# Router tiles on the place of the merged activations, router products with tokens on the partitions, late modulation products behind the first gather

## The chip, the cores and the metric

The kernel runs on one core of a Trainium2 chip. A core has TensorE (PE in the rows; PEld is its loading of weights), VectorE (DVE), ScalarE (ACT), GpSimd (POOL) and SyncE (SP), which here only issues transfers; 16 DMA engines carry them. The metric is the device time of one execution in microseconds. Everything is float32 (some products run on pairs of rounded values).

## The reference

One layer over 256 tokens of width 2048: a token mixer, then a mixture of 32 experts in four groups, each with a residual, and a last norm. The part that the change touches is the second half's beginning.

```python
mod = cond @ ada_w[l] + ada_b[l]
sh1, sc1, g1, sh2, sc2, g2 = jnp.split(mod, N_MOD, axis=-1)
...
x = x + g1[:, None, :] * mixer(h, ...)
h = modulate(rmsnorm(x, norm2_g[l]), sh2, sc2)
x = x + g2[:, None, :] * hier_moe(h, ...)
...
def hier_moe(h, wg_r, bg_r, we_r, be_r, w_gate, w_up, w_down):
    g_probs = jax.nn.softmax((hf @ wg_r + bg_r).astype(jnp.float32), axis=-1)
    g_top_p, g_top = lax.top_k(g_probs, 1)
    e_logits = (hf @ we_r + be_r).astype(jnp.float32).reshape(t, N_GROUPS, EXPERTS_PER_GROUP)
    sel = e_logits[jnp.arange(t), g_top[:, 0]]
    l_top, l_idx = lax.top_k(sel, TOP_K)
    weights = g_top_p * jax.nn.softmax(l_top, axis=-1)
    experts = (g_top * EXPERTS_PER_GROUP + l_idx).astype(jnp.int32)
    y = grouped_expert_ffn(hf, experts.reshape(-1), weights.reshape(-1), w_gate, w_up, w_down)
```

Each expert computes (silu(x w_gate) * (x w_up)) w_down with inner width 512; a token goes to two experts of one group.

## The kernel before

**Stages.** Until about 641 us the kernel computes the modulation vectors (`ada1`, `ada2`, on VectorE from 512 KB blocks) and the mixer. The mixer's last stage is the output product: for each of four blocks of 512 columns (`cb`) eight blocks `mow` of 512 KB are split into a rounded part and a rest (`hi` on ScalarE, `lo` on VectorE) and multiplied with the merged activations `mh`, `ml`. `residual(cb)` adds the result into `x1` and sums squares into `ss2`; `router_part(cb)` transposes the new columns of `x1` and multiplies them with the 36 router columns `wra` into `plg`, for the first three column blocks in the middle of the next block's products, for the last one behind all of them.

**Router.** From `plg` come the logits `lg`, from them the choice of group and experts (`onehot`, two one-hot matrices whose sum is `ma`), a rank of each token within its expert (`rk`, from three small products of `ma` with a triangular table) and a weight (`ge`, `gp`, `w1`, `w2`, `wt`).

**Experts.** The 32 experts run as eight quads of four. `gather(q)` builds a 0/1 matrix `gt` from the ranks, multiplies it with `x1` (`ph`) and evicts the 16 pieces of `hq` in turn on ScalarE and VectorE, with the second norm and the modulation applied. `quad(q)` multiplies `hq` with 16 blocks of gate and up weights (`pg`, `pu`), then with 8 blocks of down weights (`pd`). Each block is one transfer `exw` of 2048 KB, 24 a quad, 192 in all, issued by SyncE.

**Where the blocks lie.** `ring` hands out slots: five in pool `wxa` (slots 0 to 4), two in `wxb` (5, 6), and slot 7 in `wx4`, used once; after the eighth block the order is 0 to 6 again. The blocks for slots 0 to 4 are loaded in quarters during the output product (`early_some`). `wxb` lies where `mh` and `ml` lay. `wx4` and the router's tiles (pool `rt2`) lie where the ring `wp` of eight 512 KB buffers lay. The last eight of these buffers hold modulation blocks (`late`), whose products on VectorE (line 223) give the second gate `ada_state[3]`, first read in `gate2()` at the end of the first quad's gate and up products.

**What sets the order.** Inside the output product the order of SyncE is written out (`manual_schedule`). Everywhere else a scheduler places instructions by its own simulated time; each engine then runs its list in that order, and waits at the head of the list on semaphores.

## Time and profile before

| what | us |
|---|---|
| median of three runs (lowest, highest) | 1601.78 (1601.13, 1602.49) |
| the profiled execution | 1598.41 |
| its span | 1596.6 |
| TensorE busy in the span | 1233.2 (77%) |
| VectorE busy | 679.3 (43%) |
| ScalarE busy | 349.7 (22%) |
| moved by DMA | 616.27 MB, 386 GB/s in the mean |

The table gives the busy time of the whole span. The two halves have different limits, so a stage is read from its own stretch. The profile also follows the chain that ended last: 47% of the span are waits for transfers, 38% TensorE.

### The profile page before, as it was taken

The page shows a single profiled execution, that of the slowest core. Times are in us where ns is not written, and L with a number is a line of the kernel's source. Part 1 is how long each engine was busy: PE and PEld are TensorE (multiplying, and loading weights), DVE is VectorE, ACT ScalarE, POOL GpSimd, SP SyncE. Part 2 cuts the span into 40 slices and gives each one's busy share as a digit, 9 for nine tenths or more (in the row PEclk, how much of TensorE's full clock was granted, in tenths as well). Part 3 has the DMA queues.
Part 4 walks back from the last instruction along what each step waited for, and adds up shares of the span by engine and source line. Part 5 has one row for each costly group of instructions (what it writes and reads, how often), then busy time and mean ns, then how long its engine had stood idle before and what let it go on. Part 6 is the DMA issues. An engine that isn't in the chain of part 4 may idle for free.

```text
span 1596.6 us, 20401 instructions
## 1 busy us (share of the span) xinstructions
PE 1233.2 (77%) x8430; PEld 745.9 (47%) x8430; DVE 679.3 (43%) x946; ACT 349.7 (22%) x535; POOL 43.6 (3%) x40
## 2 busy tenths in 40 slices
PE   4999999999999899679657567667567566556755
PEld 3989999999899777325112112112112112111111
DVE  6989999798887966603003002002002002002002
ACT  3543355444555343112000000000000000000002
POOL 0000000300002100000000000000000000000001
PEclk9999999999999999799889779789779889777878
DMA  9999999899997899699999999999999999999996
GB/s 360 389 337 339 352 359 365 273 328 369 329 346 267 318 409 380 261 427 426 427 426 427 428 427 426 427 426 427 426 427 428 427 427 426 417 427 426 425 428 280
DMA packets 89229, 616.27 MB, mean 386 GB/s; under 512 B 10037, under 2 KB 10341, under 8 KB 64937
## 3 DMA queue, kind: packets, MB, share of 16 engines
q1 hardware_dynamic: 87700, 611.10, 95.2%
q10 hardware_dynamic: 1252, 3.48, 0.6%
q8 instruction: 68, 1.11, 0.3%
q0 software_dynamic: 176, 0.31, 0.1%
q14 instruction: 33, 0.26, 0.0%
HBM read 611.71 MB, written 2.10 MB: 384 GB/s over the span
## 4 chain that ended last, share of the span: by engine, by line
DMA 47%; PE 38%; DVE 5%; issue 1%; ACT 1%; POOL 0%; DVEq 0%; POOLq 0%; ACTq 0%
DMA w<-exw 45%; PE acc L116 23%; PE pd L116 3%; PE m L116 2%; PE ph L116 2%; PE pg L116 2%; PE pu L116 2%; DMA w<-ada 2%; DVE lo L108 1%; DVE ada L223 1%; PE po L116 1%; PE at_u L116 1%; PE pr L116 0%; DVE t L600 0%; PE sp L116 0%
## 5 line engine op out<-in xcount | busy, mean ns | idle before, releaser
L116 PE MATMUL pg<-w,hq 128*32 128x512 f32 x1024 | 185.0, 777 | 217.0 <-DMA w<-exw 217.0
L108 DVE TENSOR_TENSOR lo<-w,hi 128x1024 fp32r<-128x1024 f32 x192 | 239.5, 1253 | 42.6 <-ACT hi L107 37.8
L107 ACT CAST hi<-w 128x1024 fp32r<-128x1024 f32 x192 | 200.8, 1051 | 229.2 <-PE acc L116 179.5
L790 DVE TENSOR_TENSOR act<-act,pu 128x512 f32<-128x512 f32 x8 | 5.5, 688 | 526.2 <-PE pu L116 526.2
L116 PE MATMUL acc<-hh,hi 128*128 128x256 f32 x768 | 212.1, 280 | 0.6 <-ACT hi L107 0.6
L116 PE MATMUL acc<-hl,hi 128*128 128x256 f32 x768 | 211.3, 278 | 0.0
L116 PE MATMUL acc<-hh,lo 128*128 128x256 f32 x768 | 205.7, 279 | 2.2 <-DVE lo L108 2.1
L116 PEld LDWEIGHTS pg<-w,hq 128*32 128x32 f32 x1024 | 25.0, 118 | 363.1 <-DMA w<-exw 345.3
L116 PE MATMUL pu<-w,hq 128*32 128x512 f32 x1024 | 190.0, 793 | 0.0
L223 DVE SCALAR_TENSOR_TENSOR ada<-w,condT,ada 128x1024 f32<-128x1024 f32 x124 | 162.1, 1314 | 13.1 <-DMA w<-ada 12.2
L116 PE MATMUL pd<-w,aT 128*32 128x512 f32 x1024 | 132.2, 630 | 37.0 <-DMA w<-exw 35.5
L116 PEld LDWEIGHTS acc<-hh,hi 128*128 128x128 f32 x768 | 145.3, 189 | 2.1 <-ACT hi L107 1.4
L116 PEld LDWEIGHTS acc<-hl,hi 128*128 128x128 f32 x768 | 145.1, 189 | 0.3 <-issue 0.2
L786 ACT ACTIVATE act<-pg 128x512 f32<-128x512 f32 x8 | 4.8, 597 | 637.3 <-PE pg L116 637.3
L116 PEld LDWEIGHTS acc<-hh,lo 128*128 128x128 f32 x768 | 141.2, 189 | 3.0 <-DVE lo L108 2.6
L116 PE MATMUL po<-yb,gwt 128*128 128x512 f32 (+1 forms) x132 | 75.0, 659 | 30.4 <-DVE yb L808 19.4
L116 PEld LDWEIGHTS pu<-w,hq 128*32 128x32 f32 x1024 | 43.0, 138 | 109.9 <-issue 108.2
L116 PEld LDWEIGHTS ph<-gt,x 128*128 128x128 f32 x512 | 65.2, 195 | 43.8 <-issue 25.6
L116 PEld LDWEIGHTS pd<-w,aT 128*32 128x32 f32 x1024 | 28.7, 112 | 114.7 <-issue 60.4
L215 DVE SCALAR_TENSOR_TENSOR w<-w,condR 128x1024 f32<-128x1024 f32 x64 | 77.7, 1219 | 9.1 <-ACT condR L197 7.4
L116 PE MATMUL ph<-gt,x 128*128 128x128 f32 x512 | 74.8, 288 | 7.1 <-ACT hq L756 3.5
L815 DVE TENSOR_TENSOR x<-x,po 128x512 f32<-128x512 f32 (+1 forms) x66 | 44.3, 671 | 79.8 <-PE po L116 79.8
(246 smaller groups left out, 1481.4 us busy)
## 6 DMA issues: line engine op xcount, KB each, us to landing
w<-exw SPq DMA_DIRECT2D x186, 2048.0 KB, 30.7
w<-ada SPq DMA_DIRECT2D x192, 512.0 KB, 5.8
w<-mixw SPq DMA_DIRECT2D x64, 512.0 KB, 5.6
w<-gatew SPq DMA_DIRECT2D x64, 512.0 KB, 5.4
w<-mow SPq DMA_DIRECT2D x32, 512.0 KB, 10.2
w<-exw SPq DMA_DIRECT2D x24, 512.0 KB, 10.2
w<-fow SPq DMA_DIRECT2D x16, 512.0 KB, 5.3
w<-now SPq DMA_DIRECT2D x16, 512.0 KB, 5.1
```

What stands on the lines that cost most here:

```text
L107: nc.scalar.copy(hi, src)
L108: nc.vector.tensor_tensor(lo, src, hi.bitcast(F32), op=OP.subtract)
L116: return nc.tensor.matmul(ps, lhsT, rhs, start=start, stop=stop, skip_group_check=True)
L215: nc.vector.scalar_tensor_tensor(w, w, 1.0, condR[:, 1024 * kh:1024 * kh + 1024], op0=OP.mult, op1=OP.mult, accum_out=dst)
L223: nc.vector.scalar_tensor_tensor(a, w, condT[:, kc:kc + 1], a, op0=OP.mult, op1=OP.add)
L786: nc.scalar.activation(at_[:, 0], pg, AF.Silu)
L790: nc.vector.tensor_tensor(at_[:, 1], at_[:, 0], pu, op=OP.mult)
L815: nc.vector.tensor_tensor(x2[:, tb, c], base[:, tb, c], po[:, 0:n], op=OP.add)
```

## The change

Six things are edited.

1. The pool `rt2` of the router's tiles moves from the right side of the memory to the left, ahead of `wxb`. It now lies where `mh` and `ml` lay, slot 5 behind it on the rest of that place, and slots 6 and 7 on the buffers of `wp`.
2. In `router_part` the operands of the router product change places: the transposed tokens are the stationary operand, the 36 columns go through, one product for each half of the tokens. `plg` then holds tokens on its partitions. The copy to `lgs`, its clearing on GpSimd and the two products with the selecting table `C_SELR` go; the table goes from the constants.
3. The transposes of one column block are all issued for the first 128 tokens, then for the second, into two banks.
4. The last square sum (`cb == 3`, second half of the tokens) is taken on VectorE.
5. The late modulation products, and with them the weight steps and counts of the router, are put behind the first gather's last eviction on VectorE (`issue_after`); the subtraction for `ge` goes there too.
6. The second gather's instructions are put behind the same eviction.

```diff
     def router_part(cb):
+
+        px = [mps() for _ in range(2)]
+        for tb in range(2):
+            for pr in range(2):
+                for i in range(2):
+                    kc = 4 * cb + 2 * pr + i
+                    nc.tensor.transpose(px[pr][:, T * i + P * tb:T * i + P * tb + P],
+                                        x1[:, tb, kc * P:kc * P + P], ident)
         for pr in range(2):
-            px = mps()
+            xt2 = s4([P, 2, T], "x1t")
+            nc.scalar.copy(xt2, px[pr].rearrange("p (a b) -> p a b", a=2))
             for i in range(2):
                 kc = 4 * cb + 2 * pr + i
                 for tb in range(2):
-                    nc.tensor.transpose(px[:, T * i + P * tb:T * i + P * tb + P],
-                                        x1[:, tb, kc * P:kc * P + P], ident)
-            xt2 = s4([P, 2, T], "x1t")
-            nc.scalar.copy(xt2, px.rearrange("p (a b) -> p a b", a=2))
-            for i in range(2):
-                kc = 4 * cb + 2 * pr + i
-                mm(plg[64 * i:64 * i + 36, 0:T], wra[:, kc, :], xt2[:, i, :], kc < 2, kc >= KC - 2)
+
+                    mm(plg[:, 36 * tb:36 * tb + 36], xt2[:, i, tb * P:tb * P + P], wra[:, kc, :],
+                       kc == 0 and tb == 0, kc == KC - 1)
...
+    rt, _rt2 = pool("rt2", reuse_waits="tile")
     wxb, _wxb = pool("wxb", reuse_waits="tile")
-    rt, _rt2 = pool("rt2", "right")
     wx4, _wx4 = pool("wx4", "right", reuse_waits="tile")
 
 
-    lgs = rt.tile([P, T], F32, name="lgs")
-    nc.gpsimd.memset(lgs, 0.0)
-    for i in range(2):
-        nc.vector.tensor_copy(lgs[64 * i:64 * i + 36, :], plg[64 * i:64 * i + 36, 0:T])
...
-    pl = mps()
-    for tb in range(2):
-        mm(pl[:, 36 * tb:36 * tb + 36], lgs[:, tb * P:tb * P + P], cst[:, C_SELR:C_SELR + 36], True, True)
...
     hg = gather(0, rk, 1)
+
+    behind, first_evict = ExitStack(), last_evict[0]
+    behind.enter_context(tc.issue_after(last_evict[0].ins))
     for go in late:
         go()
...
+    behind.close()
...
-        hg = gather(q + 1, rk, q % 2)
+        with tc.issue_after(first_evict.ins) if q == 0 else ExitStack():
+            hg = gather(q + 1, rk, q % 2)
```

The scheduler orders the rest anew. On SyncE, behind the output product, the blocks `exw` of the first quad stood like this before; `w_1052` is the last modulation block, `w_1102`, `w_1103`, `w_1104` go into slots 5, 6 and 7, `w_1105` to `w_1109` into slots 0 to 4 again, and the names in brackets are the semaphores that an instruction waits for:

```order
L103 DMA w_1052_7066<-ada2 128x1024 [waits DMAHW5_49,DVE_49]
L727 DMA w_1102_7327<-exw 128x4096 [waits DMAHW6_49,PE_49]
L727 DMA w_1103_7337<-exw 128x4096 [waits DMAHW7_49,PE_49]
L727 DMA w_1104_7347<-exw 128x4096 [waits DMAHW1_49,DMAHW2_49,DMAHW0_49,DVE_49]
L869 TENSOR_LOAD nri_7273 [waits DMAHW3_49,DMAHW4_49,DMAHW2_49,DMAHW5_49,DMAHW1_49,DMAHW6_49,DMAHW0_49,DMAHW7_49,DVE_49,Activation_49]
L869 ISA x2
L727 DMA w_1105_7357<-exw 128x4096 [waits PE_49]
```

Behind these, `w_1106` to `w_1109` followed. The same place of SyncE now, where `w_1101`, `w_1102`, `w_1103` go into slots 5, 6 and 7 and `w_1104` to `w_1108` into slots 0 to 4 again:

```order
L101 DMA w_1052_7078<-ada2 128x1024 [waits DMAHW5_49,DVE_49]
L726 DMA w_1104_7366<-exw 128x4096 [waits DMAHW6_49,PE_49]
L726 DMA w_1105_7376<-exw 128x4096 [waits DMAHW7_49,PE_49]
L726 DMA w_1106_7386<-exw 128x4096 [waits DMAHW0_49,PE_49]
L726 DMA w_1107_7396<-exw 128x4096 [waits DMAHW1_49,PE_49]
L726 DMA w_1108_7406<-exw 128x4096 [waits DMAHW2_49,PE_49]
L726 DMA w_1101_7336<-exw 128x4096 [waits DMAHW3_49]
L726 DMA w_1102_7346<-exw 128x4096 [waits DMAHW4_49,DVE_49]
L726 DMA w_1103_7356<-exw 128x4096 [waits DMAHW5_49,DVE_49]
L874 TENSOR_LOAD nri_7282 [waits DVE_49]
```

The five blocks that reuse slots 0 to 4, each of which waits for the last `pu` product on the block before it in its slot, moved ahead of the three for slots 5, 6 and 7; the two of slots 6 and 7 wait for the seventh and the eighth late modulation product.

On VectorE, from the last column block's residual (`t`, `x1`) to the router's first step (`sst`), before (`ada_854` is the second gate, its `w` the late blocks):

```order
L600 TENSOR_TENSOR t_1053_7068<-acc_1011_6869,g1r_846_5907 128x512
L223 SCALAR_TENSOR_TENSOR ada_854_5950<-w_1045_7052,condT_77,ada_854_5950 128x1024
L600 TENSOR_TENSOR t_1054_7072<-acc_1012_6870,g1r_846_5907 128x512
L601 TENSOR_TENSOR x1_6285<-x1_6285,t_1053_7068 128x512
L223 SCALAR_TENSOR_TENSOR ada_854_5950<-w_1046_7054,condT_77,ada_854_5950 128x1024
L601 TENSOR_TENSOR x1_6285<-x1_6285,t_1054_7072 128x512
L223 SCALAR_TENSOR_TENSOR ada_854_5950<-w_1047_7056,condT_77,ada_854_5950 128x1024
```

Five more late products (`w_1048` to `w_1052`) and then `sst` followed. The same place of VectorE now:

```order
L598 TENSOR_TENSOR t_1053_7080<-acc_1011_6877,g1r_846_5907 128x512
L598 TENSOR_TENSOR t_1054_7084<-acc_1012_6878,g1r_846_5907 128x512
L599 TENSOR_TENSOR x1_6285<-x1_6285,t_1053_7080 128x512
L599 TENSOR_TENSOR x1_6285<-x1_6285,t_1054_7084 128x512
L601 SCALAR_TENSOR_TENSOR t_1054_7084,ss2_6323<-x1_6285 128x512
L652 TENSOR_REDUCE sst_7122<-ss2_6323 128x2
L148 TENSOR_SCALAR rv_1059_7124<-sst_7122 128x2
```

The eight late products moved away from between the sums and the router.

They stand behind the first gather's last eviction on VectorE (the first row here), among the second gather's `gt` and the weight steps:

```order
L752 TENSOR_SCALAR hq_1089_7203<-ph_1093_7243,ab2_497_3444,ab2_672_4665 128x128
L221 SCALAR_TENSOR_TENSOR ada_854_5950<-w_1045_7064,condT_77,ada_854_5950 128x1024
L221 SCALAR_TENSOR_TENSOR ada_854_5950<-w_1046_7066,condT_77,ada_854_5950 128x1024
L827 TENSOR_TENSOR ge_1067_7147<-lg_7135,mx_1063_7138 128x8
L832 TENSOR_TENSOR ex_1096_7270<-mx_1077_7165,mx_1073_7155 128x2
L853 TENSOR_REDUCE cn_7190<-cn_7190 1x1
L741 TENSOR_TENSOR gt_1143_7589<-rk_1085_7182,cst_73 128x128 x2
```

Before, this eviction was followed by the third gather's `gt`; the weight steps, the counts and the second gather's `gt` moved from within the router's chain to this place.

## Rows read from the trace of the kernel before

**Rows 1.** Page, the span in 40 equal slices: GB/s moved by the DMA engines.

```profile
GB/s 360 389 337 339 352 359 365 273 328 369 329 346 267 318 409 380 261 427 426 427 426 427 428 427 426 427 426 427 426 427 428 427 427 426 417 427 426 425 428 280
```

**Rows 2.** Stretches: length, busy us of PE, PEld, DVE, ACT, POOL, clock, DMA share, GB/s.

```profile
800.00:1000.00 200.00, 132.43 (x820) 41.17 (x824) 27.34 (x56) 9.46 (x20) 0.00 (x0) 0.87 1.01 427
...
656.00:680.00 24.00, 17.65 (x126) 9.68 (x126) 10.15 (x54) 2.61 (x7) 0.74 (x2) 0.75 0.40 157
...
641.00:656.00 15.00, 5.64 (x24) 3.04 (x22) 14.34 (x24) 4.11 (x8) 0.31 (x1) 0.61 1.01 419
...
645.00:650.00 5.00, 3.48 (x14) 1.68 (x14) 5.00 (x6) 1.90 (x4) 0.00 (x0) 0.50 1.00 426
...
560.00:640.00 80.00, 77.05 (x355) 60.08 (x354) 49.06 (x47) 31.86 (x42) 0.00 (x0) 1.00 1.01 395
...
sum 520.00, PE 506.68 PEld 479.76 DVE 468.77 ACT 244.17 POOL 33.50; mean PE 84.45 PEld 79.96 DVE 78.13 ACT 40.69 POOL 5.58
```

**Rows 3.** SyncE: issues by start and duration; then one of its waits (us, times, longest).

```profile
637.31 12.34 SPq L727 DMA_DIRECT2D w<-exw  x3
...
669.82 28.61 SPq L727 DMA_DIRECT2D w<-exw  x11
...
SPq L727 <- DVE ada L223: 7.1, 1, 7.1
```

**Rows 4.** TensorE in order of time, 640 to 676: start, duration, what, [idle before].

```profile
641.31 0.39 PE L116 MATMUL acc<-lo,mh 128*128 128x512 f32 x1
...
645.77 1.54 PE L610 MATMUL m<-cst,x 128*128 128x128 f32 x6 [1.28 <-DVE x L601]
647.40 1.93 PE L116 MATMUL plg<-x1t,wr 128*36 128x256 f32 x8
...
660.59 1.76 PE L116 MATMUL m<-ma,cst 128*128 128x32 f32 x10 [5.15 <-DVE w L833]
...
668.71 1.03 PE L116 MATMUL pu<-w,hq 128*32 128x512 f32 x8
...
671.65 1.04 PE L116 MATMUL pu<-w,hq 128*32 128x512 f32 x8
```

**Rows 5.** The other engines in order of time; then four pieces of the chain.

```profile
640.83 0.69 DVE L600 TENSOR_TENSOR t<-acc,g1r 128x512 f32<-128x512 f32 x1 [3.97 <-PE acc L116]
...
642.63 0.68 DVE L600 TENSOR_TENSOR t<-acc,g1r 128x512 f32<-128x512 f32 x1
643.23 0.68 DVE L601 TENSOR_TENSOR x<-x,t 128x512 f32<-128x512 f32 x1
...
645.03 0.68 DVE L601 TENSOR_TENSOR x<-x,t 128x512 f32<-128x512 f32 x1
...
645.63 7.26 DVE L223 SCALAR_TENSOR_TENSOR ada<-w,condT,ada 128x1024 f32<-128x1024 f32 x6
...
646.76 1.17 ACT L613 COPY x1t<-m 128x512 f32<-128x512 f32 x2 [0.23 <-PE m L610]
...
653.00 0.31 POOL L645 MEMSET lgs<- 128x256 f32 x1 [102.79 <-DVE ada L223]
...
655.48 0.42 DVE L656 SCALAR_TENSOR_TENSOR lg<-m,rr,cbr 128x36 f32<-128x36 f32 x2 [0.30 <-PE m L116]
...
656.29 0.07 DVE ge L678
...
660.45 0.08 DVE w L833
...
662.78 0.66 DVE gt L742 x3
...
666.15 0.43 PE pt L767 x2
```

**Rows 6.** TensorE at full clock: router products at 580, transposes at 622.

```profile
579.64 1.06 PE L116 MATMUL plg<-x1t,wr 128*36 128x256 f32 x8
...
621.52 0.82 PE L610 MATMUL m<-cst,x 128*128 128x128 f32 x6
```

More of the change, by code (lines that the diff above doesn't have):

```diff
@@ L25 @@
 WIN = (0, 32, 96, 128)
-C_ID, C_LT, C_ONE, C_SELR, C_IOTA, C_DESC, C_THR, C_END = 0, 128, 256, 384, 420, 452, 484, 492
+C_ID, C_LT, C_ONE, C_IOTA, C_DESC, C_THR, C_END = 0, 128, 256, 384, 416, 448, 456
 V_SH1, V_SC1, V_SH2, V_SC2, V_N1, V_N2, V_GB = 0, 16, 32, 48, 64, 80, 96
@@ L38, in const_table @@
     t[:, C_ONE:C_ONE + P] = 1
-    for j in range(2):
-        t[64 * j + np.arange(36), C_SELR + np.arange(36)] = 1
     t[:, C_IOTA:C_IOTA + 32] = np.arange(32)
@@ L601, in residual @@
             nc.vector.tensor_tensor(x1[:, tb, c], x1[:, tb, c], tmp, op=OP.add)
-            nc.scalar.activation(tmp, x1[:, tb, c], AF.Square, accum_out=ss2[:, tb, cb:cb + 1])
-    def router_part(cb):
+            if cb == 3 and tb:
+                nc.vector.scalar_tensor_tensor(tmp, x1[:, tb, c], 1.0, x1[:, tb, c], op0=OP.mult, op1=OP.mult,
+                                               accum_out=ss2[:, tb, cb:cb + 1])
+            else:
+                nc.scalar.activation(tmp, x1[:, tb, c], AF.Square, accum_out=ss2[:, tb, cb:cb + 1])
+    def router_part(cb):
+        px = [mps() for _ in range(2)]
[5 more added lines that the diff above has]
+                                        x1[:, tb, kc * P:kc * P + P], ident)
         for pr in range(2):
-            px = mps()
+            xt2 = s4([P, 2, T], "x1t")
+            nc.scalar.copy(xt2, px[pr].rearrange("p (a b) -> p a b", a=2))
             for i in range(2):
@@ L650, in build @@
     rs2 = rstd_of(rt, sst, 2)
-    pl = mps()
-    for tb in range(2):
-        mm(pl[:, 36 * tb:36 * tb + 36], lgs[:, tb * P:tb * P + P], cst[:, C_SELR:C_SELR + 36], True, True)
     lg = rt.tile([P, 2, 36], F32, name="lg")
     for tb in range(2):
-        nc.vector.scalar_tensor_tensor(lg[:, tb, :], pl[:, 36 * tb:36 * tb + 36], rs2[:, tb:tb + 1], cbr,
+        nc.vector.scalar_tensor_tensor(lg[:, tb, :], plg[:, 36 * tb:36 * tb + 36], rs2[:, tb:tb + 1], cbr,
                                        op0=OP.mult, op1=OP.add)
@@ L677, in build @@
     ge, gsum, gp = sm([2, 4], "ge"), sm([2], "gs"), sm([2], "gp")
-    nc.vector.tensor_tensor(ge, gl, gm[:, :, None].to_broadcast([P, 2, 4]), op=OP.subtract)
     off, e1, e2 = sm([2, 4], "off"), sm([2, 32], "e1"), sm([2, 32], "e2")
@@ L752, in gather @@
                 if i % 2:
-                    nc.vector.tensor_scalar(hq[:, kc, :], ph[:, i, :], A2[:, kc:kc + 1], B2[:, kc:kc + 1],
+                    last_evict[0] = nc.vector.tensor_scalar(hq[:, kc, :], ph[:, i, :], A2[:, kc:kc + 1], B2[:, kc:kc + 1],
                                             op0=OP.mult, op1=OP.add)
@@ L817, in quad @@
                         tail(x2, tb, cb + i, c, cb < 3)
-    late_x2 = []
+    late_x2, last_evict = [], [None]
     hg = gather(0, rk, 1)
+    behind, first_evict = ExitStack(), last_evict[0]
+    behind.enter_context(tc.issue_after(last_evict[0].ins))
     for go in late:
         go()
+    nc.vector.tensor_tensor(ge, gl, gm[:, :, None].to_broadcast([P, 2, 4]), op=OP.subtract)
     nc.scalar.activation(ge, ge, AF.Exp)
@@ L918, in build @@
     nc.sync.dma_start(out[:, 0, 1024:D], x2[:, 0, 1024:D])
-    for e in (_pe, _ac, _rt2, _wxb, _wxa, _rt, _x1p, _r0, _cp):
+    for e in (_pe, _ac, _wxb, _rt2, _wxa, _rt, _x1p, _r0, _cp):
         e.close()
```

## The prediction

> **What bounds the kernel now.** I read first the page's slices, then the busy times by stretch, then the SyncE queue with its waits, then the engines in order of time between 640 and 676 us.
>
> The slices [rows 1] show two halves: up to slice 16 the rate changes from 260 to 410 GB/s, in slice 17 it is 261, from there on 426 to 428. The stretch 800 to 1000 us gives the reason: DMA share 1.01 at 427 GB/s, TensorE busy 132 of 200 us; from 560 to 640 us TensorE was busy 77 of 80 [rows 2]. So the second half lasts as long as its bytes take: every weight block (128x4096 float32, 2.097 MB) costs 2.097 MB / 427 GB/s = 4.91 us, and nothing that TensorE does faster there is seen. What can be won or lost is time in which the DMA engines stand idle ahead of it. There is one such place: 656 to 680 us runs at 157 GB/s [rows 2], so (1 − 157/427) × 24 = 15.2 us of transfer are missing. The stream is back at full rate in effect at 656 + 15.2 = 671.2 us.
>
> Why it stops: SyncE issues all expert blocks of the main path, in its own order [rows 3]. Five (slots 0 to 4) were loaded during the output product. At 637.3 us it begins to issue three more (slots 5, 6, 7; the third waits 7.1 us for a late modulation product), and the 15 us × 419 GB/s = 6.29 MB between 641 and 656 us [rows 2] are exactly these three. Then all eight slots are full. The next block needs slot 0 free, which it is when TensorE has used the first block: its last `pu` product ends at 668.71 + 1.03 = 669.74 us [rows 4], SyncE's next issue stands at 669.82 [rows 3]; full rate is reached in effect 1.5 us after the product.
>
> **What the change does, part by part.**
>
> *The order on SyncE decides the sign.* In the built program the five blocks that reuse slots 0 to 4 stand ahead of the three for slots 5, 6 and 7. SyncE waits at the head of its list: one late product held it 7.1 us [rows 3], with all that stood behind. So after the modulation blocks it now waits for the first `pu` products to end, and no other engine issues these blocks. The three that ran from 641 to 656 us under the router move behind the restart. That costs 3 × 4.91 = **+14.7 us**. Slots 6 and 7 now lie where the late modulation blocks lie, which DVE uses only after the first gather; that would hold those two back in any order. Slot 5 needs nothing but the end of the mixer's products, so its early load is lost to the order alone.
>
> *The router chain gets shorter,* and with it the restart comes earlier [rows 4, 5]:
> - Six late products between the last residual and the router take 7.26 us of DVE, 1.21 each; two more stand between the residual's steps. POOL's clearing of `lgs` waited for them until 653.0. Now the second `t` follows the last mixer product (641.31 + 0.39 = 641.7), and two sums at a pitch of 0.6 (643.23 after 642.63) end at 643.7, against 645.71 before. Of eight transposes four can follow the first sum, four the second; at 1.54/6 = 0.26 each the last ends near 645.0. Two copies on ACT, 1.17 together, end at about 645.2 and 645.8.
> - The router products of the last column block were 8 with 256 columns in 1.93. Now they are 16 with 36 columns; the nearest row is `m<-ma` (128 columns of weights, 32 columns through them, same clock), 1.76/10 = 0.18 each, so 2.8: from 645.2 to about 648.3 with the copy between. `lgs`, its copies and the selecting product are gone. The scale's five small DVE steps and the square that moves from ACT to DVE lie under transposes and products. `lg` starts at about 648.5 against 655.48: −7.0.
> - Further on, seven small weight steps stood between the choice's steps, 0.07 to 0.12 each, 0.6 in all (first `ge`, last `w`): −0.6. Two of the four `gt` steps ahead of the first gather belong to the second, 0.22 each: −0.4. The transposes `pt`, 0.43, go behind the gather: −0.4.
>
> Sum −8.4, to be held between −7 and −12 (the upper end is the first rival). The first block is used at 661.3, the stream is in effect back at 662.8. I price products at half clock: the granted clock stood at 0.50, the 1.2 GHz level, from 645 us on [rows 2], after a pause from 641.7, and that pause stays.
>
> *Net at the restart:* −8.4 + 14.7 = **+6.3 us**.
>
> *Router products inside the output product.* Three of the four groups run there, where TensorE is busy 77 of 80 us [rows 2], so their time is on the path. Eight products of 256 columns take 1.06 us at full clock [rows 6]. Sixteen of 36 columns load 128 columns of weights each. Bounds: 16 × 0.088 = 1.4 (the 0.18 above, halved with the clock) and 16 × 0.137 = 2.2 (six transposes in 0.82 us, [rows 6]), so +0.3 to +1.1 a group; a gain would need under 0.066 each, less than any row with such weights. I take 0.65, between: **+1.9 us**. Here a rule bears on it. The Trainium skill (TensorE: Matmul & The Clock Gate, Back-to-back issue gap) gives about 81 ns to each load-and-product pair of 128 columns in a stream; by it a group costs 1.3, the term is +0.7 and the time 1608.8. The transposes, such pairs in fp32, took 137 ns here, so I stay with the rows.
>
> *At nothing:* the late products cost DVE 10 to 13 us after the gather (eight at 1.21 and the weight steps among them), while TensorE works on blocks that have landed. The cover lasts until the six blocks that are issued ahead of slot 6's have passed, 662.8 + 6 × 4.91 = 692.3. The gather should end near 677 (five blocks at 671.65 − 668.71 = 2.94 us [rows 4], then the last evictions), the seventh late product near 688. If that slips past 690 the stream waits: 0 to +3. The order of the first stages moves too (the table of constants is smaller, and the scheduler shifted products by some places): 0, within −3 and +3.
>
> **The sum.** +6.3 + 1.9 = +8.2. The profiled execution took 1598.41 us, its span 1596.6 with 1.8 around it; by it the changed kernel takes 1606.6. The median of the three runs, 1601.78, lies 3.4 above, and I carry the change to it: 1601.78 + 8.2 = **1610.0 us**.
>
> **Rivals.**
> - *TensorE stays at 2.4 GHz through the router.* Last transposes, router products, ranks and first gather products, some 7 us at half clock, would save about 3.6: 1606.4. For: the work is denser than before. Against: the pause after 641.7, and DVE works alone for some 4 us between `lg` and the ranks.
> - *Not slower: the early stages give it back.* From 40 to 560 us TensorE idles 520 − 506.7 = 13.3 us [rows 2]. If products that had to wait now stand behind ones that are ready, part of that goes; from 8.2 us on the sign turns, at two thirds, 8.9, the time is 1601.1. For: many products moved there. Against: nothing is ready sooner than it was, and as many moved the other way.
> - *Slot 6 late:* the last evictions end after 680, the stream waits another 3 us at 692: 1613. For: the gather's last seven pieces alternate with evictions on two engines. Against: five blocks' products and six transfers lie over it.
> - *The chain does not move* (something else holds the router until 653): only the costs are left, 14.7 + 1.9: 1618.4. Against: the new DVE order has nothing between the sums and the router.
>
> **How the numbers follow.** Forecast 0.66, full clock 0.08, early stages 0.14, slot 6 late 0.08, chain unmoved 0.04. 0.2% is 3.2 us, about what a measurement of this kernel can tell from no change. Slower by more: 0.63 + 0.06 + 0.08 + 0.04 = 0.81; within: 0.03 + 0.02 + 0.07 = 0.12; faster by more: 0.07, half of the early-stage case. The range leaves out the early-stage case and the unmoved chain and takes in the bounds of the other terms: 1604.5 to 1615.5.
>
> **What would show it.** Right: no transfers from about 641 to 662 us, the first expert issue of the second half behind 661; `lg` near 648.5, the first `pu` done near 661; TensorE waiting for slot 5's block until about 692; 427 GB/s from 665 us to the end. Wrong: transfers between 645 and 660 us; a first `pu` done before 655 (there the shorter chain pays for the three blocks); a last mixer product that ends before 639 or after 646; a second gap near 692.

## The result and the profile after

The changed kernel took 1624.2 us (median of four runs, 1622.7 to 1625.3), the kernel before beside it 1602.1: a ratio of 1.0132, 95% interval 1.0111 to 1.0152, 22 us slower. Slower was forecast, 1610.0 with a range up to 1615.5; the time lies 9 us above the range. Between the two profiled executions the spans differ by more, 1622.8 − 1596.6 = 26.2 us, because the profiled execution of before was a quick one.

The slices of the page after, to be held against [rows 1]: slice 16 fell from 261 to 162 GB/s, and the rate behind it is the old one.

```profile
GB/s 367 380 321 362 336 334 360 258 312 324 334 310 322 268 382 381 162 427 426 427 427 428 428 427 427 429 427 427 429 427 426 429 427 428 420 428 427 426 429 282
```

The busy times by stretch after (columns as in [rows 2]: length, busy us of PE, PEld, DVE, ACT, POOL, clock, DMA share, GB/s):

```profile
800.00:1000.00 200.00, 131.65 (x816) 41.40 (x816) 20.79 (x46) 9.48 (x20) 0.00 (x0) 0.84 1.01 428
661.00:685.00 24.00, 15.43 (x88) 9.89 (x86) 10.46 (x43) 3.18 (x8) 0.51 (x2) 0.64 0.06 14
645.00:660.00 15.00, 15.00 (x75) 12.68 (x75) 6.27 (x6) 4.22 (x5) 0.00 (x0) 1.00 0.98 377
40.00:553.90 513.90, 497.94 (x4079) 472.70 (x4077) 446.95 (x526) 235.15 (x340) 31.99 (x24) 0.99 0.92 325
553.90:661.00 107.10, 102.67 (x500) 84.23 (x500) 73.41 (x69) 41.05 (x51) 3.25 (x1) 1.00 0.96 370
```

From 661 to 685 us the transfers stand still (14 GB/s); before, the three blocks ran in the first 15 us behind the mixer. SyncE after, its issues, then one of its waits (us, times, longest), as in [rows 3]:

```profile
642.75 14.08 SPq L101 DMA_DIRECT2D w<-ada  x9
682.60 115.75 SPq L726 DMA_DIRECT2D w<-exw  x29
```

```profile
SPq L726 <- DVE ada L221: 13.1, 1, 13.1
```

The first expert block of the second half is issued at 682.60, at the end of the first `pu` product (680.68 + 1.84 = 682.52), as forecast. TensorE in order of time, as in [rows 4]:

```profile
660.93 0.39 PE L114 MATMUL acc<-lo,mh 128*128 128x512 f32 x1
...
662.79 1.16 PE L613 MATMUL m<-cst,x 128*128 128x128 f32 x8 [1.47 <-DVE x L599]
664.47 2.96 PE L114 MATMUL plg<-wr,x1t 128*128 128x36 f32 x16 [0.51 <-ACT x1t L617]
672.57 1.76 PE L114 MATMUL m<-ma,cst 128*128 128x32 f32 x10 [5.14 <-DVE ma L686]
...
678.98 1.94 PE L114 MATMUL pg<-w,hq 128*32 128x512 f32 x8
680.68 1.84 PE L114 MATMUL pu<-w,hq 128*32 128x512 f32 x8
```

VectorE from the logits to the end of the choice, before and then after, and the first gate products before:

```profile
655.48 0.42 DVE L656 SCALAR_TENSOR_TENSOR lg<-m,rr,cbr 128x36 f32<-128x36 f32 x2 [0.30 <-PE m L116]
...
660.22 0.23 DVE L687 TENSOR_TENSOR ma<-eq,eq 128x64 f32<-128x64 f32 x1
```

```profile
667.47 0.42 DVE L656 SCALAR_TENSOR_TENSOR lg<-plg,rr,cbr 128x36 f32<-128x36 f32 x2 [1.48 <-PE plg L114]
...
672.20 0.22 DVE L686 TENSOR_TENSOR ma<-eq,eq 128x64 f32<-128x64 f32 x1
```

```profile
667.49 1.40 PE L116 MATMUL pg<-w,hq 128*32 128x512 f32 x8
```

Most of it looks as the prediction drew it, shifted: the mixer's last product ends at 661.3 instead of 641.7. That shift is not the output product. The first product of that stage in the two traces (before, then after), with the wait ahead of it:

```profile
535.45 0.47 PE L116 MATMUL acc<-hi,mh 128*128 128x512 f32 x1 [1.82 <-POOL g L543]
```

```profile
553.94 0.47 PE L114 MATMUL acc<-hi,mh 128*128 128x512 f32 x1 [1.86 <-POOL g L541]
```

18.5 us were lost before the output product began, in stages of which the change edits no line. The busy times of the same stretches before:

```profile
40.00:535.45 495.45, 484.33 (x4081) 461.00 (x4079) 444.84 (x526) 234.99 (x340) 30.25 (x24) 0.99 0.93 338
535.45:641.70 106.25, 101.10 (x476) 79.92 (x476) 73.87 (x70) 41.03 (x51) 3.25 (x1) 1.00 0.97 375
```

4081 records of TensorE before, 4079 after: the same products. They keep it busy 13.6 us longer (497.9 against 484.3), and it idles 4.8 us more (16.0 against 11.1). Two things make up most of the 13.6 us. Neighbouring products of 256 columns (some 3,400 pairs whose starts lie at most 135 ns apart) follow each other after 116.9 ns in the mean instead of 114.2, 9 us in all. And the granted clock at its lower level cost 7.1 us of full speed in this stretch instead of 3.5.

So the span can be cut into four parts: the start of the output product, its length, the chain from its last product to the end of the first `pu`, and the rest. Before: 535.5 + 106.2 + 28.0 + 926.9 = 1596.6. After: 553.9 + 107.4 + 21.2 + 940.3 = 1622.8. The experiments are read in this table; each row is one profiled execution, the ratio is to the kernel before on the same chip.

| kernel | ratio, 95% interval | output product starts | mixer ends | chain | rest | span |
|---|---|---|---|---|---|---|
| before | 1 | 535.5 | 641.7 | 28.0 | 926.9 | 1596.6 |
| after | 1.0132 (1.0111 to 1.0152) | 553.9 | 661.3 | 21.2 | 940.3 | 1622.8 |
| e1_table | 1.0042 (1.0028 to 1.0055) | 537.1 | 644.4 | 19.6 | 940.7 | 1604.7 |
| e2_small_before | 1.0093 (1.0073 to 1.0114) | 551.3 | 657.3 | 29.0 | 925.2 | 1611.5 |
| e3_slot5_first | 1.0020 (1.0008 to 1.0031) | 540.4 | 648.1 | 21.2 | 936.9 | 1606.2 |
| e4_late_free | 0.9993 (0.9982 to 1.0005) | 538.4 | 645.9 | 26.4 | 926.0 | 1598.3 |
| e5_wide_table | 1.0129 (1.0114 to 1.0145) | 554.6 | 662.0 | 19.9 | 937.8 | 1619.6 |
| e6_567_first | 1.0160 (1.0141 to 1.0178) | 539.2 | 647.0 | 19.5 | 960.1 | 1626.6 |
| e7_late_inside | 0.9959 (0.9946 to 0.9973) | 540.5 | 650.7 | 19.5 | 926.0 | 1596.2 |
| e8_before_late_inside | 0.9977 (0.9964 to 0.9989) | 540.6 | 649.0 | 21.0 | 927.0 | 1597.0 |
| e9_new_order_old_place | 1.0123 (1.0100 to 1.0146) | 548.9 | 656.5 | 21.2 | 940.8 | 1618.5 |
| e10_old_order_new_place | 1.0083 (1.0063 to 1.0104) | 548.1 | 655.7 | 19.5 | 938.1 | 1613.4 |
| e11_gap32 | 1.0028 (1.0014 to 1.0041) | 548.3 | 659.5 | 21.2 | 925.3 | 1605.9 |
| e12_gap64 | 1.0051 (1.0032 to 1.0070) | 551.8 | 662.0 | 21.1 | 925.1 | 1608.2 |

One execution is not a median: before, e1, e3, e4 and e6 do the same work in the same order up to the output product, and begin it between 535.5 and 540.4. Differences of a few us between single rows are scatter; the medians carry the verdicts.

### The profile page after: what moved, and what is told of

The parts are those of the page before. It is cut to its first block, busy times and chain, and to the rows that moved or that the text cites. A ratio compares the mean times of both kernels' runs of the same rounds, so it can differ in the third digit from the quotient of the medians.

```text
span 1622.8 us, 20436 instructions
## 1 busy us (share of the span) xinstructions
PE 1245.3 (77%) x8458; PEld 765.4 (47%) x8458; DVE 682.0 (42%) x946; ACT 348.8 (21%) x533; POOL 44.7 (3%) x39
## 4 chain that ended last, share of the span: by engine, by line
DMA 49%; PE 20%; DVE 7%; issue 2%; ACT 1%; DVEq 0%; ACTq 0%
DMA w<-exw 42%; PE acc L114 6%; DMA w<-ada 5%; PE pd L114 3%; PE ph L114 3%; PE pg L114 3%; DVE ada L221 3%; PE pu L114 2%; DVE lo L106 2%; PE po L114 1%; DMA w<-gatew 1%; DMA w<-now 1%; PE plg L114 0%; PE pr L114 0%; PE m L114 0%
## 5 line engine op out<-in xcount | busy, mean ns | idle before, releaser
L114 PE MATMUL pg<-w,hq 128*32 128x512 f32 x1024 | 180.4, 771 | 221.7 <-DMA w<-exw 221.7
L114 PE MATMUL acc<-hh,lo 128*128 128x256 f32 x768 | 209.2, 282 | 3.2 <-DVE lo L106 3.2
L114 PE MATMUL po<-yb,gwt 128*128 128x512 f32 (+1 forms) x132 | 70.4, 621 | 30.4 <-DVE yb L807 19.4
L114 PEld LDWEIGHTS ph<-gt,x 128*128 128x128 f32 x512 | 68.6, 203 | 51.0 <-issue 23.0
L114 PE MATMUL ph<-gt,x 128*128 128x128 f32 x512 | 78.5, 297 | 14.3 <-DVE gt L743 7.7
```

The costliest lines, as they stand in the source:

```text
L114: return nc.tensor.matmul(ps, lhsT, rhs, start=start, stop=stop, skip_group_check=True)
```

## The experiments

### Was it the table of constants? (e1_table, e2_small_before)

The change drops the selecting columns from the table of constants. In the traces TensorE and VectorE follow another order from 122 us on, although the first edited products run some 440 us later. Two kernels cross the two things:

```diff
 changed kernel -> e1_table
-C_ID, C_LT, C_ONE, C_IOTA, C_DESC, C_THR, C_END = 0, 128, 256, 384, 416, 448, 456
+C_ID, C_LT, C_ONE, C_IOTA, C_DESC, C_THR, C_END = 0, 128, 256, 420, 452, 484, 492
 kernel before -> e2_small_before
-C_ID, C_LT, C_ONE, C_SELR, C_IOTA, C_DESC, C_THR, C_END = 0, 128, 256, 384, 420, 452, 484, 492
+C_ID, C_LT, C_ONE, C_IOTA, C_DESC, C_THR, C_END = 0, 128, 256, 384, 416, 448, 456
...
-        mm(pl[:, 36 * tb:36 * tb + 36], lgs[:, tb * P:tb * P + P], cst[:, C_SELR:C_SELR + 36], True, True)
+        for j in range(2):
+            mm(pl[:, 36 * tb:36 * tb + 36], lgs[:, tb * P:tb * P + P], cst[:, 64 * j:64 * j + 36], j == 0, j == 1)
```

> The changed kernel with one line undone: the table of constants keeps its old width of 492 columns (36 of them are zeros), so that its first transfer is as large as before. By the order of its instructions every engine then does the whole mixer in the order of the kernel before, and everything behind it in the order of the changed kernel. Theory A, the order of the first stages carries the part of the loss that the prediction took as 0: of the 26.2 us between the two profiled spans, 19.7 lie ahead of the mixer's last product, and about 2.4 of these are the router products inside the output product; 17.3 go, the mixer's last product ends near 644, the median falls from 1624.2 to about 1607 (1605 to 1611), still slower than before. Theory B, the loss in the mixer comes from something else of the change (the new place of the router's tiles, the products of the late blocks): the mixer's end stays near 661 and the time at 1624.

Measured: 1607.6 us (six runs), ratio 1.0042. One line, which touches nothing that is computed, took 16.5 us off the changed kernel by the medians of two rounds, 14 by the ratios. TensorE of e1_table in order of time, then its stretches:

```profile
644.00 0.39 PE L114 MATMUL acc<-lo,mh 128*128 128x512 f32 x1
647.54 1.98 PE L114 MATMUL plg<-wr,x1t 128*128 128x36 f32 x16 [0.51 <-ACT x1t L617]
...
662.78 1.18 PE L114 MATMUL pu<-w,hq 128*32 128x512 f32 x8
```

```profile
40.00:537.11 497.11, 483.31 (x4075) 459.35 (x4074) 445.65 (x526) 234.87 (x340) 29.93 (x24) 1.00 0.93 337
...
650.00:655.00 5.00, 0.34 (x2) 0.37 (x2) 3.89 (x19) 0.00 (x0) 0.00 (x0) 0.78 0.00 0
```

This kernel is the one that the prediction had summed up. Its span lies 1604.7 − 1596.6 = 8.1 us above that of before, against +8.2 forecast; its median, 1607.6, lies within the range. The mixer's end is 2.7 later, the chain 8.4 to 8.5 shorter, the rest 13.8 longer. That the sum agrees to the tenth is luck: 1.7 of the 8.1 us are a later start of the output product, within its scatter, and by the ratio the kernel is 6.7 us slower (4.5 to 8.8).

> The kernel before with the table of constants cut to 456 columns as in the changed kernel; the selecting product reads two pieces of the identity instead (four small products for two, about +0.4 us), the result is the same. The mixer's order is then the changed kernel's, everything else is of before. Theory A: the mixer's last product ends near 659 instead of 641.7, and the time is 1602.1 + 17.3 + 0.4 = about 1620 (1617 to 1623). Theory B: 1602 to 1603, mixer's end near 642.

Measured: 1616.2 us, ratio 1.0093; the mixer's last product ends at 656.90 + 0.39 = 657.3.

```profile
656.90 0.39 PE L114 MATMUL acc<-lo,mh 128*128 128x512 f32 x1
```

The kernel before loses 15 us by the smaller table alone, a little under the 17 to 18 expected. What the table does is shown; by which way it does it, order or something else, is the subject of the last five kernels.

### What the order on SyncE costs (e3_slot5_first, e6_567_first)

```diff
 e1_table -> e3_slot5_first
     wx4, _wx4 = pool("wx4", "right", reuse_waits="tile")
+    w5 = wxb.tile([P, 4096], F32, tag=f"w{NA}", bufs=1, name=nm("w"))
+    w5_load = nc.sync.dma_start(w5, A["exw"][0, NA])
+    early.append(w5)
+    loads = [w5_load]
...
-                    eng.dma_start(w[:, n * i:n * i + n], src[:, n * i:n * i + n])
+                    loads.append(eng.dma_start(w[:, n * i:n * i + n], src[:, n * i:n * i + n]))
...
+        if q == 0:
+            for i, j in ((1, 7), (2, 7), (3, 0), (4, 0), (5, 0), (6, 0), (7, 0)):
+                tc.add_manual_dep(loads[i].ins, loads[j].ins.name,
+                                  mybir.DependencyInfo(mybir.DependencyClass.NoSync, mybir.DependencyReason.DATA), reason="order")
```

> The kernel of e1_table with one load moved: the first block for slot 5 is issued directly behind the last modulation block, ahead of the five reloads of slots 0 to 4; the blocks for slots 6 and 7 stay behind those. If each block that is held back by the order costs its transfer, 4.91 us come back against e1_table. Of that the stream may give up to 3 us back a little later, since the block for slot 6 is now due after five blocks instead of six and waits for the seventh late product (in the changed kernel 27 us behind the first pu product, five blocks are 24.5). So 2 to 4.9 us under e1_table, about 1603. Rival, the order of SyncE costs nothing and the loss behind the mixer lies in the late products: same time as e1_table, and SyncE waits longer for the late products.

Measured: 1605.5 us (ten runs), ratio 1.0020 against 1.0042, 2 to 3.5 us less. In the table the rest falls from 940.7 to 936.9: 3.8 of the 4.9 us of one block came back. (One execution each; the rest also moves with the rate of the transfers, which from 800 to 1200 us was 427 GB/s in both.) SyncE:

```profile
648.08 0.33 SPq L651 DMA_DIRECT2D w<-exw  x1
669.33 86.58 SPq L731 DMA_DIRECT2D w<-exw  x22
```

The block for slot 5 goes out as soon as the mixer has ended, 21 us ahead of the next one. The order on the queue, not the memory, had held it.

In e6_567_first the first quad's loads are only put behind that of slot 5, and the scheduler then issues those for slots 6 and 7 next:

```diff
 e3_slot5_first -> e6_567_first
...
-        if q == 0:
-            for i, j in ((1, 7), (2, 7), (3, 0), (4, 0), (5, 0), (6, 0), (7, 0)):
...
-        quad(q, *hg, x1 if q == 0 else None, ring_get if q < NQ - 2 else last_ring)
+        with tc.issue_after(w5_load.ins) if q == 0 else ExitStack():
+            quad(q, *hg, x1 if q == 0 else None, ring_get if q < NQ - 2 else last_ring)
```

> The kernel of e1_table with the three first blocks for slots 5, 6 and 7 issued in this order ahead of the reloads of slots 0 to 4, while the late products stay behind the first gather. The prediction said that slots 6 and 7 would be held back in any order, since they lie on the late blocks. If so, SyncE now stands at its head until the seventh late product, some 27 us behind the first pu product, with all reloads queued behind; slot 5 alone lands early. The stream restarts some 25 us later than in e1_table and gains 4.9 for slot 5: about 20 us more, near 1628 (1622 to 1631). Rival, the late products are early enough in any order: as e3_slot5_first or better, 1596 to 1605.

Measured: 1628.4 us, ratio 1.0160, the slowest of all. SyncE's wait for the late product, then the stretch in which nothing was moved:

```profile
SPq L730 <- DVE ada L221: 43.1, 1, 43.1
```

```profile
653.00:692.00 39.00, 24.63 (x163) 14.73 (x162) 17.74 (x56) 6.44 (x12) 0.51 (x2) 0.76 0.05 14
```

One wait of 43.1 us at the head of the list, 39 us at 14 GB/s, and a rest that is 960.1 − 940.7 = 19.4 us longer than in e1_table (about 20 expected). With the late products behind the gather, the blocks for slots 6 and 7 cannot come early; the order that the scheduler chose was the better of the two.

### What putting the late products behind the gather is worth (e4_late_free)

```diff
 e1_table -> e4_late_free
     behind, first_evict = ExitStack(), last_evict[0]
-    behind.enter_context(tc.issue_after(last_evict[0].ins))
```

> The kernel of e1_table without the edge that puts the late products and the weight steps behind the first gather (edit 5 undone; place of the router's tiles and operands as in the changed kernel). SyncE then issues the blocks for slots 5, 6 and 7 ahead of the reloads, as before, and VectorE does the late products among the sums and the router's first steps, as before. Theory: the 14.7 us of the three blocks come back, and most of the 6.9 us that the router's chain had won go: lg waits for the last late product, near 655 to 657. Time 1602.1 + 2.4 of router products in the output product, less at most 2 for the dropped lgs steps: 1602.5 to 1604.5. Rival, the chain was shortened by the operands and the new place and not by the late products: lg near 650, time near 1597.

Measured: 1600.8 us, ratio 0.9993: no difference from the kernel before, and a little under the time expected. VectorE, the last late product and the logits:

```profile
656.58 1.28 DVE L221 SCALAR_TENSOR_TENSOR ada<-w,condT,ada 128x1024 f32<-128x1024 f32 x1
...
658.83 0.42 DVE L656 SCALAR_TENSOR_TENSOR lg<-plg,rr,cbr 128x36 f32<-128x36 f32 x2
```

`lg` stands 12.9 us behind the mixer's end (5.2 in e1_table, 13.8 before), and the chain is 26.4 again. The rest is back at 926.0. So edit 5 gives the chain 6.8 us and takes 14.7 from the stream; the other edits bring some 1.7 us of the chain and cost 1.2 us in the output product.

### Getting the short chain without its price (e7_late_inside, e8_before_late_inside)

The late products wait for their blocks, and these were loaded last. Two kernels load them inside the output product, and eight quarters of expert blocks in their stead behind the last weight block:

```diff
 e1_table -> e7_late_inside; the same lines in the kernel before -> e8_before_late_inside
-                early_some(max(0, i - 5) * 4 * NA // 26 - max(0, i - 6) * 4 * NA // 26)
+                early_some(max(0, i - 5) * 12 // 26 - max(0, i - 6) * 12 // 26)
...
                 late = [ada_load() for _ in range(len(ada_q))]
+                early_some(len(quarters))
...
-LEAD, PACE = 3, 14
+LEAD, PACE = 3, 22
```

> The kernel of e1_table with the last eight modulation blocks loaded and multiplied inside the output product (22 blocks there instead of 14); in exchange eight of the twenty quarters of the expert blocks for slots 0 to 4 are loaded behind the last weight block of the mixer. The bytes ahead of the router stay the same, but nothing of the late products is left behind the mixer, and slots 5, 6 and 7 are free at once. Theory: the chain of e1_table (19.6 to 21 us from the mixer's last product to the first pu product, 28.0 in the kernel before) without its price of 14.7 on SyncE: 1601.5 - 8.4 + 1.2 to 2.7 = 1594 to 1596. Rival, eight more blocks in the ring of eight buffers hold up the weight blocks of the output product: its end moves by 5 or more, the time is 1600 or above.

Measured: 1595.3 us, ratio 0.9959 (0.9946 to 0.9973): 6.5 us faster than the kernel before and, by the ratios, some 28 faster than the changed one. The stretches behind its mixer:

```profile
651.00:666.00 15.00, 7.12 (x42) 6.12 (x42) 9.12 (x40) 2.15 (x6) 0.51 (x2) 0.65 0.83 351
666.00:672.00 6.00, 5.82 (x37) 2.71 (x40) 0.82 (x2) 1.03 (x3) 0.00 (x0) 0.74 0.19 38
```

The three blocks run under the router at 351 GB/s, and only the 6 us behind them are nearly empty. Against 427 GB/s, (1 − 351/427) × 15 + (1 − 38/427) × 6 = 8.1 us of transfer are missing behind the mixer, instead of the 15.2 of the kernel before. The output product takes 110.1 us instead of 107.4, the smaller part of the rival.

> The same exchange of loads in the kernel before, with none of the change's edits. The logits then no longer wait for the late products (653.0 on GpSimd, 655.48 for lg), only for the router products, the two copies to lgs and the selecting product: lg near 651, 4.5 us earlier, time 1601.5 - 4.5 = 1597 (1595 to 1599). If the time falls to that of e7_late_inside, the edits of the change (operands and place) bring nothing of their own once the late products are gone; if it stays at 1601, the late products did not set the router's start in the kernel before.

Measured: 1598.0 us, ratio 0.9977. The logits stand 6.6 us behind the mixer's end, 7 us earlier than before, as they no longer wait for late products:

```profile
655.63 0.42 DVE L657 SCALAR_TENSOR_TENSOR lg<-m,rr,cbr 128x36 f32<-128x36 f32 x2 [1.10 <-PE m L116]
```

The intervals of e7 and e8 overlap: most of the gain comes from the exchange of loads. What the change's own edits add to it is 3 us by the ratios, with an uncertainty as large.

### By which way the table moves the mixer (e5, e9 to e12)

A larger table was the first test of order against size.

```diff
 changed kernel -> e5_wide_table
-C_ID, C_LT, C_ONE, C_IOTA, C_DESC, C_THR, C_END = 0, 128, 256, 384, 416, 448, 456
+C_ID, C_LT, C_ONE, C_IOTA, C_DESC, C_THR, C_END = 0, 128, 256, 456, 488, 520, 528
```

> The changed kernel with the table of constants widened by zeros to 528 columns, so that its first transfer is 264 KB, larger than the 246 KB of the kernel before (228 KB in the changed kernel). By its order of instructions the mixer is then nearly the changed kernel's (SyncE and GpSimd the same, 42 of some 4000 rows of TensorE differ), not that of before (328 differ). Theory A, the order is what costs: the mixer's last product near 657 to 661, time 1617 to 1625. Theory B, it is the width of the table itself (a small transfer lands at another time and shifts the first stages): a wider table gives at most the time of e1_table, 1607 or less.

Measured: 1622.2 us, ratio 1.0129. A transfer that is larger than before is as slow as one that is smaller. That fitted theory A, the order. But the traces held something that this theory has no place for. At 70 to 84 us the order of the engines does not differ yet, TensorE does nothing but products of 256 columns, one behind another, at a granted clock of 1.00 (the 2.4 GHz level); and the count of them differs. e1_table, then the changed kernel:

```profile
70.00:84.00 14.00, 14.00 (x126) 14.00 (x125) 11.82 (x16) 8.52 (x11) 0.00 (x0) 1.00 0.99 379
```

```profile
70.00:84.00 14.00, 14.00 (x122) 14.00 (x122) 11.35 (x16) 8.52 (x11) 0.00 (x0) 1.00 0.98 370
```

A product's record lasts 0.28 us, so 14.28/126 = 113.3 ns from one to the next in e1_table, and 14.28/122 = 117.0 in the changed kernel. A count holds whole products only, so such a figure is good to 1 ns; from the first start to the last in the same stretch the means are 113.3 and 116.7. What differs there is where the data lie. The table is the first tile on the left side of the memory; with 36 columns less every tile behind it lies 160 bytes of each partition lower (the columns are 144 bytes, and a tile begins at a multiple of 32), among them the operands `hh` and `hl` of these products, while the buffers on the right side (`w`, `hi`, `lo`) stay. An unused tile behind the table separates the two:

```diff
 changed kernel -> e9_new_order_old_place (36 columns)
 e1_table -> e10_old_order_new_place (32 columns)
 e7_late_inside -> e11_gap32 (8 columns), e12_gap64 (16 columns)
     cst = cp.tile([P, C_END], F32, name="cst")
+    gap = cp.tile([P, 36], F32, name="gap")
```

> The changed kernel with an unused tile of 36 columns behind the table of constants: the table, its transfer and the order of every engine stay exactly the changed kernel's, while every tile behind the table lies on the address that it had in the kernel before (160 bytes of each partition further on). The traces so far allow two readings of the longer mixer. Around 80 us, where the order of instructions does not differ yet and the granted clock is 1.00 in both, TensorE starts a product of 256 columns every 113.3 ns in e1_table and every 116.6 ns in the changed kernel; 4080 products at 3.3 ns more are 13.5 us. Theory C, the addresses: the pitch goes back to 113.3 ns, the mixer's last product to 644 to 648, the time to about 1608 (1605 to 1611). Theory A, the order: the pitch near 80 us may be what it likes, the mixer still ends near 660 and the time stays 1622 to 1625.

> The counterpart: the kernel of e1_table with an unused tile of 32 columns behind the table, so that the order of every engine stays exactly that of e1_table, while the tiles behind the table lie on the addresses of e5_wide_table (128 bytes of each partition further on), whose products had the long pitch. Theory C, the addresses: pitch 116 to 118 ns, the mixer's end near 658, time 1620 to 1624. Theory A, the order: pitch and time of e1_table, 1607.

The pitch went with the place, in both. e9, then e10:

```profile
70.00:84.00 14.00, 14.00 (x126) 14.00 (x125) 11.82 (x16) 8.52 (x11) 0.00 (x0) 1.00 1.00 375
```

```profile
70.00:84.00 14.00, 14.00 (x121) 14.00 (x120) 11.45 (x15) 8.29 (x11) 0.00 (x0) 1.00 0.99 365
```

113.3 ns in e9, 118.0 in e10 (117.8 by the starts). By the starts, the distance is 113.3 ns in each of the eight kernels at the place of before, in either order, 116.7 in both at 160 bytes less (the changed kernel, e2_small_before) and 117.8 in both at 128 bytes more (e5, e10). The place sets the distance. The times did not go with the place alone. e9 took 1620.5 us (ratio 1.0123), e10 1614.5 (1.0083). Each theory has half:

| | place of before | another place |
|---|---|---|
| order of e1_table | 1.0042 | 1.0083 (e10) |
| order of the changed kernel | 1.0123 (e9) | 1.0132 (after), 1.0129 (e5) |

The new place alone costs 0.41%, 6.6 us; the new order alone 0.81%, 13 us; both together 0.9%, 14 us. They don't add, and the table leaves two things open. The 160 bytes less of the change itself were tried in the new order only, where giving the place back (e9) is worth 0.09%, which the intervals do not tell from nothing. And with the order the size of the table's transfer differs too (228 KB in e9, 246 in e1_table); e5, with 264 KB, is slow as well, so size alone would have to cost both ways. The stretch ahead of the output product, e9 and then e10:

```profile
40.00:548.94 508.94, 491.17 (x4079) 465.08 (x4078) 447.36 (x526) 235.01 (x340) 32.73 (x24) 0.99 0.91 329
```

```profile
40.00:548.08 508.08, 496.56 (x4077) 472.24 (x4076) 446.22 (x526) 235.00 (x340) 30.97 (x24) 0.99 0.92 329
```

In e10 TensorE is busy 496.6 us against 483.3 in e1_table, and idles no more than there (11.5 against 13.8). Of these 13.3 us some 10 are the longer distance: over the 3,400 pairs of the whole stretch it is 117.3 ns in the mean against 114.3. The others are a spell at half clock that e1_table does not have there, (0.29 + 0.39) × 5 = 3.4 us of full speed:

```profile
310.00:315.00 5.00, 3.03 (x23) 2.60 (x27) 4.33 (x6) 3.64 (x6) 3.34 (x3) 0.71 0.47 136
315.00:320.00 5.00, 5.00 (x36) 4.59 (x31) 4.72 (x6) 2.31 (x10) 1.27 (x1) 0.61 0.74 239
```

The output product, whose operands `mh`, `ml`, `hi` and `lo` lie on the right side and stay, takes 107.3 to 107.6 us in e1_table, the changed kernel, e5, e9 and e10, at three places and in both orders. In e9 TensorE idles 4.0 us more than in e1_table (17.8) and is busy 7.9 us more. A part of that is one wait of e9 and what followed it:

```profile
319.48 0.58 PE L114 MATMUL acc<-yfh,lo 128*128 128x256 f32 x1 [2.98 <-DVE lo L106]
```

```profile
315.00:320.00 5.00, 2.02 (x20) 1.65 (x20) 4.06 (x4) 2.54 (x6) 1.66 (x1) 0.87 0.67 245
320.00:325.00 5.00, 5.00 (x26) 5.00 (x25) 5.00 (x8) 1.04 (x1) 0.00 (x0) 0.50 0.78 230
325.00:330.00 5.00, 5.00 (x42) 5.00 (x42) 4.62 (x5) 1.05 (x1) 0.00 (x0) 0.95 0.88 301
```

TensorE stood 2.98 us for a rest `lo`, and the granted clock fell to 0.50, the 1.2 GHz level, for what sums to (0.13 + 0.50 + 0.05) × 5 = 3.4 us of full speed. The changed kernel, in the same order, has the same wait and the same loss behind it; before and in e1_table the rows of TensorE show no wait between 310 and 330 us:

```profile
324.55 0.58 PE L114 MATMUL acc<-yfh,lo 128*128 128x256 f32 x1 [2.75 <-DVE lo L106]
```

VectorE in e9 shows what stands ahead of that `lo`: a modulation product that waited for its block.

```profile
315.94 1.28 DVE L222 SCALAR_TENSOR_TENSOR ada<-w,condT,ada 128x1024 f32<-128x1024 f32 x1 [1.97 <-DMA w<-ada]
317.14 2.29 DVE L106 TENSOR_TENSOR lo<-w,hi 128x1024 fp32r<-128x1024 f32 x1
```

In the changed kernel that product waited 2.38 us. How much of the delay is this wait was not tried: `hi` came late as well, behind other steps on ScalarE. Idle time (4.0 us), half clock (3.4) and a distance of 114.9 ns against 114.3 in the mean (2) are some 9.4 of the 11.8 us by which e9 begins the output product later than e1_table. The other 2.4 stay open.

> The kernel of e7_late_inside with an unused tile of 8 columns behind the table of constants: order unchanged on TensorE, every tile behind the table 32 bytes of each partition further on. The places tried so far are 0 (pitch 113.3 ns near 80 us), 160 bytes less (117) and 128 bytes more (118). If the place of the kernel before is only one of many good ones, pitch and time stay (113 ns, 1594 to 1597). If it is a lucky one, the pitch goes to 117 or 118 and the time to 1595.3 + 7 = about 1602, as between e1_table and e10_old_order_new_place.

> The same with 16 columns, 64 bytes of each partition further on. If the pitch went by the place modulo 64 bytes, it would be that of e7_late_inside here (113.3 ns, 1594 to 1597); 128 bytes more were slow, which speaks against that. If the place of the kernel before is a lucky one: 117 to 118 ns, about 1602.

```profile
70.00:84.00 14.00, 14.00 (x121) 14.00 (x120) 11.30 (x15) 8.37 (x11) 0.00 (x0) 1.00 1.00 368
```

```profile
70.00:84.00 14.00, 14.00 (x120) 14.00 (x118) 11.83 (x16) 7.61 (x11) 0.00 (x0) 1.00 0.97 361
```

Measured: e11 1607.3 us (1.0028), e12 1610.0 (1.0051), against 1595.3 (0.9959) without the gap; the pitches are 118.0 and 119.0 ns by the count, 118.4 and 120.0 by the starts. Of the five places tried, that of the kernel before is the lucky one: the distance is longer at all four others, and the time is longer at the three that were tried with the order held (32, 64 and 128 bytes more). The cost was larger than the 7 us that I had taken from e10: by the ratios 11 us for 32 bytes and 15 for 64.

## Why the prediction was wrong, and where it was right

**The step that failed** stands at the end of its last item under "At nothing": "The order of the first stages moves too (the table of constants is smaller, and the scheduler shifted products by some places): 0, within −3 and +3". It measured +18.5 us between the two profiles; between the changed kernel and e1_table it is 16.5 by the medians and 14 by the ratios. Three things were wrong in it. The price was put at 0 without a reason. The bound of ±3 came from no row either. And it had one name, order, for two mechanisms: the smaller table also moves the place of every tile behind it, of which the step says nothing. The runs showed in its place that the size of the table alone moves the mixer's end (e1_table, e2_small_before), and that either mechanism costs by itself: another order, with the smaller table, at the old place 13 us (e9), another place in the old order 6.6 us (e10, 128 bytes more). Why the products follow each other more slowly at another place, and a part of what the order costs, stay open.

**The rival on the early stages** was the right place with the wrong sign. It asked how much of 13.3 us of idle time could be given back and left out that as much could be lost. Most of the loss was no idle time at all: TensorE was busy 13.6 us longer and idle 4.8 us more.

The other steps, each by the parts of the table:

- *Order on SyncE, +14.7:* the rest behind the first `pu` product grew by 13.4 in the changed kernel and by 10.9 to 13.9 in the four others with the same order on SyncE (e1, e5, e9, e10). Right, a little over. The two low ones, e5 and e10, moved their blocks at 429 GB/s instead of 427 from 800 to 1200 us, which is 1.9 of the 3 us there alone. That slots 6 and 7 would be held back in any order: shown by e6. That slot 5's load was lost to the order alone: shown by e3, 3.8 of 4.9 us.
- *The chain, −8.4, between −7 and −12:* −6.8 in the changed kernel, −8.4 in e1_table. The two levels that the new chain takes in the table, 19.5 to 19.9 and 21.1 to 21.2, go with the clock: the sixteen router products took 1.98 us in e1_table, where half clock came only behind 650 us, and 2.96 in the changed kernel. The rival of full clock holds for a part of the chain in some executions and is worth 1.6 us, not 3.6. So the −8.4 of e1_table is no proof of the sum, which was priced at half clock. Its parts came out otherwise: up to `lg` −8.6 in e1_table and −7.6 in the changed kernel, where −7.0 stood; behind `lg` +0.1 and +0.8, where −1.4 stood. The seven weight steps, put at −0.6, had cost nothing: from the start of `lg` to the end of `ma` VectorE took 4.97 us before and 4.95 after. And the first gate and up products, of which the sum has nothing, took 3.5 us in the changed kernel and 2.9 in e1_table, with half clock in them, against 2.25 before.
- *Router products in the output product, +1.9:* the stage grew from 106.2 to 107.4, by 1.1, and by 1.0 to 1.6 in the four kernels that share the old order (e1, e3, e4, e6). Inside its bounds of 0.9 to 3.3, near the lower one.
- *Late products and slot 6, 0 to +3:* SyncE stood 13.1 us for the seventh late product, and the stream showed no second gap, since six blocks were queued ahead of it. In e3, with five, the block came back 1 us short; whether the late product took that is not shown.
- *The sum:* 13.4 − 6.8 + 1.1 + 18.5 = 26.2. Without the last term it is 7.7, against 8.2.

The signs listed as right were there, but some 20 us later: no transfers between the mixer's end and the first `pu`, the first expert issue at its end, the full rate behind. The sign listed as wrong, a last mixer product that ends after 646, came at 661.

## What to carry to other kernels

Where a scheduler and a stack of tiles lie between the text and the chip, an edit to a constant is an edit to everything behind it: compare order and addresses of the stages that you did not touch, and if either moved, hold them (pad the table, keep its size) before you judge the edit. A gain on a chain counts only with the queue that feeds the next stage in view: here 7 us of router were bought with 13 us of idle DMA engines, and an exchange of loads gave the first without the second. And a pitch, the count of equal products in a full stretch, shows a slower engine where busy shares show nothing.

## What the runs showed of the hardware that I had not expected

- The distance between two products of TensorE depends on where the tiles on the left side lie, the operands `hh` and `hl` among them. The same products in the same order at the same granted clock of 1.00 followed each other (mean of the starts, 70 to 84 us) after 113.3 ns at the place of the kernel before, 116.7 at 160 bytes less, 118.4 at 32 bytes more, 120.0 at 64 and 117.8 at 128. Which accesses meet was not tried.
- The Trainium skill (TensorE: Matmul & The Clock Gate, Back-to-back issue gap) gives 262 cycles for 256 columns at full clock as the gap of products by themselves, by estimate 109 ns. The stretches read here do not reach it, the nearest is 113.3.
- A single pause of 2.98 us inside a busy stage was followed by half clock (e9), 3.4 us of lost work on top of the pause. In the changed kernel a pause of 2.75 us was followed by the same.
- The start of the output product scatters by 5 us between executions, 535.5 to 540.4 over five kernels with the same order up to there. A prediction made from one profile inherits that; carrying the change to the median was right.
